# A planner that is told of a shorter latency between an operation and its dependents, and a layer boundary with another place in its queues

## The chip, the cores and the metric

The kernel runs on one core of a Trainium2 chip, as one program with one launch. The metric is the device time of one execution in microseconds (us), as the median of several runs; lower is better.

## What is computed

Two layers of a decoder trunk over 512 tokens of width 1024, batch 1, in float32. Cut to what matters:

```python
for l in range(DEPTH):                       # DEPTH = 2
    h = rms_norm(x, pre_norm_g[l])
    u = einsum('bsd,de->bse', h, w_in[l])    # 3424 columns, five groups
    # latent attention (MLA): low-rank query and key/value latents, rotary key
    q, k, v = from_latents(rms_norm(c_q) @ w_uq, rms_norm(c_kv) @ w_ukv)
    o_a = causal_softmax_attention(q, k, v)
    o_b = stick_breaking_attention(q, k, v)  # sigmoids, products from the right
    o_c = moba_attention(q, k, v, rel_bias)  # with 512 tokens plain causal softmax + bias
    o_d = conformer_conv(u_conv)             # gate, 31 taps, layer norm, swish, pointwise
    y = concat([o_a, o_b, o_c, o_d]) * silu(u_gate)
    y = einsum('bse,ed->bsd', y, w_out[l])
    x = x + rms_norm(y, post_norm_g[l])
```

## The kernel before

All matrices are split into a high and a low part (`hH`, `hL` for the normalised input, `w` for weights, `yH`, `yL` for the mixed output), and every product is three matmuls. Tokens are in four tiles of 128 (`t` = 0 to 3). Weights come in units of 128 x 512: a DMA into one of three `raw` buffers, a cast on ACT (L358) that makes the high part, and a subtraction on DVE or POOL (L363) that makes the low part. Six `w` buffers are used in turn.

No order of work is written out by hand. The program is a set of small tasks, written as generators. Each yields the engine that its next instruction needs, an estimated duration and the time at which its inputs are ready. `Flow.run` keeps a model of every engine's clock, and again and again issues the operation with the lowest key: its start in the model, plus a weight of the engine (`WT`: 0.078 for PE, 0.691 for DVE, 0.094 for POOL, 0 for ACT, 0.496 for SP) times the priority of its task (`PR`). What depends on an operation is taken to be ready at the operation's modelled end plus `LAG`. So the table of numbers sets the order in which instructions stand in each engine's queue, and each queue is then worked off in that order on the chip.

The names that matter:

- `x_new` (L1173 to L1197) closes a layer for one token tile: the square sum on ACT (L472), the sum and the power (L464 on DVE, L466 on POOL), four updates of `xt` on DVE (L1193). `boundary` (L519) normalises that tile for the next layer: another square sum (L472), L464, L466, then `h` on DVE (L527), transposes on PE (L537 `tr`), the split into `hH` on ACT (L544) and `hL` on DVE (L547).
- Products of the input projection: `lat` of a token tile (L580, 24 matmuls of 352 columns), the value chunk `vC` (L580 `acc`, 96 matmuls of 256 columns, 24 for a token tile), the others (L647, 512 columns, 24 for a half chunk).
- MLA's preparation: transposes of the latents (L693), `cq` from them (L760 on ACT, L762 on DVE), queries (L710, five matmuls a head), keys (L720) and values (L743), rotary embedding of queries on DVE or POOL (L779, L781, L786; L783 copies the rotary key). L720 and L743 use the weight unit `ukv`.
- Attention: scores (L1032 for MLA, L1037 otherwise) go to one of two PSUM buffers `sc`. DVE reads a score tile with the mask and takes the row maximum (L1064), ACT takes the exponential (L1072) and scales it (L1077), PE transposes the result (L1082), and L1098 multiplies with the values. A score buffer comes free when L1064 is through.
- The output projection is L1126. PE's other work is always issued as filler around attention.

Of the kernel before, what the change touches and what calls it, by code (L numbers as in the profile page):

```python
# [64 lines left out]
AORDER = (('mla', 0), ('mla', 1), ('moba', 0), ('moba', 1), ('sb', 0), ('sb', 1))  # L65


LAG = 330
CONV_NS = 205000.0
TAP_LATE = 40  # L70
TAP_EARLY = 100
# [3 lines left out]
BPN = 360.0  # L75
FBS = 1
SPARE0 = 1500.0
PR = {'low': 155, 'hs': 50, 'lat': 50, 'ev': 50, 'vev': 60, 'va': 65, 'cq': 40, 'q': 35, 'cn': -40, 'pw': -5, 'pv': 12, 'ys': 85, 'ye': 70, 'xn': 20, 'xs': 10, 'bd': 10, 'pre': 70, 'u0': 0, 'u1': 0, 'u2': 21, 'u3': 1}
BANKS = {"acc": 6, "sc": 2}
ENGINE = {"dvx": "dve", "plm": "pool"}  # L80
PORT = ("dvx", "pool")
# [8 lines left out]
class Flow:  # L90
# [19 lines left out]
    def spawn(self, prio, gen):  # L110
        task = [prio, self.n, gen, None]
        self.n += 1
        self.tasks.append(task)
        self.tasks.sort(key=lambda a: a[:2])
        self.resume(task, None)
# [7 lines left out]
    def run(self):  # L123
        while self.tasks:
# [17 lines left out]
            else:  # L142
# [6 lines left out]
                if len(q) > 3 and q[3]:  # L149
                    self.table = q[3]  # L150
                self.resume(task, (q[0], end + LAG) if isinstance(task[3], list) else end + LAG)

# [22 lines left out]
    def drop(self, buf, t):  # L175
        buf.at = max(buf.at, t)
        buf.uses -= 1
        if buf.uses == 0:
            self.free[buf.tag].append((buf.at, buf.idx))
            if buf.also:  # L180
                self.drop(buf.also, buf.at)
# [31 lines left out]
def trunk(ctx, tc, x, pre_g, w_in, w_sm, vecs, w_out, post_g, rel_bias, consts, onehot, out):  # L213
# [119 lines left out]
    def splitter():  # L333
        for key, src, n, nu, nk, w1 in feed:
            for kq in range(nu):
                raw, t0 = yield lambda: fl.ev.get(("raw", key, kq))
                r3 = raw.ap.rearrange("p (k c) -> p k c", k=nk)
                if w1:
                    raw.uses = nk
                    for j in range(nk):  # L340
# [4 lines left out]
                        A.copy(bh.ap, r3[:, j, :])  # L345
                        spawn(PR["low"], low_part(key, k, raw, r3[:, j, :], bh.ap, bl.ap, n, max(t, bl.at), [bh, bl]))
                else:
# [10 lines left out]
                    A.copy(wH, r3)  # L358
                    spawn(PR["low"], low_part(key, kq, raw, r3, wH, wL, 2 * n, t, b))

    def low_part(key, i, raw, r3, h, lo, n, t, b):
        e, t = yield from either(n, t)
        e.tensor_tensor(lo, r3, h.bitcast(F32), ALU.subtract)  # L363
        drop(raw, t)
        units[key, i] = (h, lo, t, b)
# [69 lines left out]
    def warm_up():  # L435
# [3 lines left out]
        while ("h", 0, 0, 0) not in fl.ev or fl.clock[pEng] < fl.ev["h", 0, 0, 0] - 600:  # L439
            te = yield pEng, 107 if t > WARM_AT else 213, t  # L440
            PE.matmul(b.ap[:, :256], zb[:, :P], zb[:, P : P + 256], start=True, stop=True)
            t = te - LAG
        drop(b, te)
# [88 lines left out]
    def flip_h(l, t, a, h, hp, tt, nb=4):  # L532
# [6 lines left out]
        sl = (slice(None), slice(a * nb, a * nb + nb), slice(t * P, (t + 1) * P))  # L539
        spawn(PR["hs"] + (0 if l else FBS) * t, h_split(l, t, a, nb, sl, tr3, tr, tp))  # L540

    def h_split(l, t, a, nb, sl, tr3, tr, tp):
        te = yield aEng, act(nb * P), tp
        A.copy(hs[0][sl], tr3)  # L544
        mark(("hH", l, t, a), te)
        te = yield vEng, dve(nb * P), te
        V.tensor_tensor(hs[1][sl], tr3, hs[0][sl].bitcast(F32), ALU.subtract)  # L547
        drop(tr, te)
        if nb < 4:
            mark(("hL", l, t, a), te)  # L550
            if ("hL", l, t, a ^ 1) in fl.ev:
                h_done(l, t, a // 2, te)
        else:
            h_done(l, t, a, te)

    def first_latents():
# [9 lines left out]
        for n, (k, x_, i) in enumerate(seq):  # L566
# [3 lines left out]
            PE.matmul(o, hs[x_][:, k, :P], (wh, wl)[i], start=n == 0, stop=n == len(seq) - 1)  # L570
        spawn(PR["lat"], latent_norm(0, 0, a, te))

    def tok_mm(o, wf, l, t, r, last):
        tc_ = slice(t * P, (t + 1) * P)
        for k in range(KT):
            th = yield from wait(("h", l, t, k // 4))
            wh, wl, tw, b = yield from wf(k)
            for i, (a, w) in enumerate(((hs[0], wh), (hs[0], wl), (hs[1], wh))):
                te = yield pEng, pe(wh.shape[-1]), max(th, tw, r)
                PE.matmul(o, a[:, k, tc_], w, start=k == 0 and i == 0, stop=k == KT - 1 and i == 2)  # L580
            last(k, b, te)
        return te

    def latents(l, t):
# [12 lines left out]
        te = yield from tok_mm(o, wf, l, t, a.at, last)  # L597
        spawn(PR["lat"], latent_norm(l, t, a, te))

    ckv = {}  # L600

    def latent_norm(l, t, a, te):
        zb = yield from take("qk", f"ckv{t}", C_SB)
        z = zb.ap
        t0 = yield aEng, act(C_SB), max(te, zb.at)
        A.copy(z, a.ap[:, :C_SB])
        drop(a, t0)
        ss = small("ssl", 2)
        jk = yield from take("yt", "jk", QR)
        t1 = yield aEng, acta(QR), max(t0, jk.at)  # L610
        A.activation(jk.ap, z[:, :QR], AF.Square, accum_out=ss[:, 0:1], scale=1.0 / math.sqrt(QR))
        t1 = yield aEng, acta(KVR), t0
        A.activation(jk.ap[:, :KVR], z[:, QR + RD :], AF.Square, accum_out=ss[:, 1:2], scale=1.0 / math.sqrt(KVR))
        drop(jk, t1)
        t2 = small("kr", 2 * RD, 2)
        kr = z[:, QR : QR + RD]
        tcs = yield from wait("cst")
        t0 = max(t0, tcs)
        td = yield xEng, 100, t0
        V.tensor_tensor(t2[:, :RD], kr, ck[:, t, :], ALU.mult)  # L620
        td = yield xEng, 85, t0
        V.tensor_tensor(t2[:, RD : RD + 16], kr[:, 16:], sk[:, t, 0:16], ALU.mult)
        td = yield xEng, 85, t0
        V.tensor_tensor(t2[:, RD + 16 :], kr[:, :16], sk[:, t, 16:], ALU.mult)
        r, t1 = yield from rsq(ss, 2, 1.0, t1)
        td = yield xEng, 100, td
        V.tensor_tensor(kr, t2[:, :RD], t2[:, RD:], ALU.add)
        td = yield xEng, dve2(QR), t1
        V.tensor_scalar(z[:, :QR], z[:, :QR], r[:, 0:1], None, ALU.mult)
        td = yield xEng, dve2(KVR), t1  # L630
        V.tensor_scalar(z[:, QR + RD :], z[:, QR + RD :], r[:, 1:2], None, ALU.mult)
        ckv[l, t] = zb
        mark(("ckv", l, t), td)

    def feat_chunk(l, c, evac, pre=None):
        key = (l, c)
        for m in range(2):
# [4 lines left out]
            for k in range(KT):  # L642
# [5 lines left out]
                if m == 1:  # L648
                    drop(b, te)
            spawn(PR["ev"], evac(m, a, te))  # L650

# [703 lines left out]
```

## Time and profile before

| | |
|---|---|
| median of 3 runs | 546.67 us (546.61 to 549.04) |
| the profiled execution | 547.47 us |
| its span, first to last instruction | 545.7 us |
| outside the span | 1.8 us |
| mean granted TensorE clock | 0.994 |
| PE busy | 532.7 us |
| DVE, ACT, POOL busy | 407.4, 362.8, 214.6 us |

The profiled execution is 0.8 us longer than the median. "Busy" counts a matmul from its start to its modelled end, so that the engine's pace is better read from the distance between two starts.

### The profile page before, as it was taken

The page shows a single profiled execution, that of the slowest core. Times are in us where ns is not written, and L with a number is a line of the kernel's source. Part 1 is how long each engine was busy: PE and PEld are TensorE (multiplying, and loading weights), DVE is VectorE, ACT ScalarE, POOL GpSimd, SP SyncE. Part 2 cuts the span into 40 slices and gives each one's busy share as a digit, 9 for nine tenths or more (in the row PEclk, how much of TensorE's full clock was granted, in tenths as well). Part 3 has the DMA queues.
Part 4 walks back from the last instruction along what each step waited for, and adds up shares of the span by engine and source line. Part 5 has one row for each costly group of instructions (what it writes and reads, how often), then busy time and mean ns, then how long its engine had stood idle before and what let it go on. Part 6 is the DMA issues. An engine that isn't in the chain of part 4 may idle for free.

```text
span 545.7 us, 9448 instructions
## 1 busy us (share of the span) xinstructions
PE 532.7 (98%) x3181; PEld 461.6 (85%) x3181; DVE 407.4 (75%) x914; ACT 362.8 (66%) x862; POOL 214.6 (39%) x255
## 2 busy tenths in 40 slices
PE   9999899999999999999998999999999999999995
PEld 5998678888888898899997967788888889989995
DVE  4667875788999988953687597558899998897243
ACT  5647898348995748654674699825699766674531
POOL 5823111572435643422241032048424566243321
PEclk9999899999999999999999999999999999999999
DMA  7423230344314263133763112323452423413245
GB/s 283 151 94 111 79 96 23 95 134 124 109 40 118 76 171 107 40 111 99 264 187 118 40 38 68 107 78 83 129 152 62 114 80 94 138 40 98 61 165 178
DMA packets 31025, 59.47 MB, mean 109 GB/s; under 512 B 4033, under 2 KB 5953, under 8 KB 30978
## 3 DMA queue, kind: packets, MB, share of 16 engines
q1 hardware_dynamic: 30978, 58.88, 35.8%
q8 instruction: 25, 0.41, 0.3%
q14 instruction: 22, 0.18, 0.1%
HBM read 49.17 MB, written 5.51 MB: 100 GB/s over the span
## 4 chain that ended last, share of the span: by engine, by line
PE 89%; DVE 5%; ACT 2%; POOL 1%; issue 1%; DMA 1%; SPq 0%; POOLq 0%; DVEq 0%; ACTq 0%
PE acc L647 40%; PE acc L1126 16%; PE acc L580 8%; PE pv L1098 5%; PE lat L580 5%; PE tr L1082 5%; PE sc L1037 4%; PE sc L1032 2%; DMA raw<-in_w_in_dram 1%; PE acc L968 1%; POOL wl L363 1%; DVE kT L783 1%; PE tr L537 1%; PE acc L710 1%; DVE qT L786 1%
## 5 line engine op out<-in xcount | busy, mean ns | idle before, releaser
L647 PE MATMUL acc<-hH,w 128*128 128x512 f32 x640 | 212.1, 403 | 0.0
L363 POOL TENSOR_TENSOR w<-raw,w 128x512 fp32r<-128x512 f32 x85 | 110.4, 1305 | 151.7 <-ACT w L358 126.2
L647 PEld LDWEIGHTS acc<-hH,w 128*128 128x128 f32 x640 | 119.5, 189 | 24.0 <-issue 0.4
L647 PE MATMUL acc<-hL,w 128*128 128x512 f32 x320 | 129.8, 406 | 0.0
L358 ACT CAST w<-raw 128x512 fp32r<-128x512 f32 x130 | 79.8, 622 | 42.1 <-PE acc L647 16.8
L893 DVE SCALAR_TENSOR_TENSOR cv<-cx,vec,cv 128x512 f32<-128x512 f32 x116 | 87.1, 751 | 2.4
L1126 PE MATMUL acc<-w,yH 128*128 128x256 f32 x416 | 75.3, 282 | 0.0
L647 PEld LDWEIGHTS acc<-hL,w 128*128 128x128 f32 x320 | 60.5, 189 | 11.4
L1126 PEld LDWEIGHTS acc<-w,yH 128*128 128x128 f32 x416 | 64.5, 189 | 0.4
L1126 PE MATMUL acc<-w,yL 128*128 128x256 f32 x208 | 59.0, 284 | 0.2
L363 DVE TENSOR_TENSOR w<-raw,w 128x512 fp32r<-128x512 f32 x45 | 33.4, 743 | 26.8 <-ACT w L358 26.7
L580 PE MATMUL acc<-w,hH 128*128 128x256 f32 x256 | 49.3, 287 | 1.9 <-DVE w L363 1.9
L382 DVE TENSOR_TENSOR pt<-tr,pt 128x128 fp32r<-128x128 f32 (+3 forms) x96 | 45.6, 484 | 5.8 <-ACT pt L376 4.5
L1082 PE MATMUL tr<-cst,p 128*128 128x128 f32 x240 | 42.2, 276 | 0.6 <-ACT p L1077 0.6
L580 PEld LDWEIGHTS acc<-w,hH 128*128 128x128 f32 x256 | 40.1, 189 | 2.8 <-DVE w L363 2.1
L376 ACT CAST pt<-tr 128x128 fp32r<-128x128 f32 (+3 forms) x96 | 39.8, 423 | 3.8 <-PE tr L1082 2.7
L1082 PEld LDWEIGHTS tr<-cst,p 128*128 128x128 f32 x240 | 30.2, 141 | 13.5 <-ACT p L1077 4.8
L1126 PEld LDWEIGHTS acc<-w,yL 128*128 128x128 f32 x208 | 39.3, 189 | 0.7 <-DVE yL L379 0.7
L580 PE MATMUL acc<-w,hL 128*128 128x256 f32 x128 | 36.4, 284 | 0.0
L1077 ACT ACTIVATE p<-p,s 128x128 f32<-128x128 f32 (+3 forms) x64 | 35.2, 562 | 1.8 <-DVE s L1075 1.8
L1072 ACT ACTIVATE p<-zb,s 128x128 f32<-128x128 f32 (+2 forms) x64 | 35.9, 561 | 0.3
L1161 POOL TENSOR_TENSOR yr<-yr,g 128x512 f32<-128x512 f32 x12 | 16.6, 1387 | 39.0 <-ACT jk L472 39.0
(179 smaller groups left out, 1019.8 us busy)
## 6 DMA issues: line engine op xcount, KB each, us to landing
raw<-in_w_in_dram SPq DMA_DIRECT2D x96, 256.0 KB, 2.7
raw<-in_w_out_dram SPq DMA_DIRECT2D x32, 256.0 KB, 2.6
xt<-in_x_dram SPq DMA_DIRECT2D x8, 512.0 KB, 4.2
raw<-in_w_sm_dram SPq DMA_DIRECT2D x8, 256.0 KB, 3.7
bias<-scratch SPq DMA_DIRECT2D x8, 256.0 KB, 2.9
m<-m SPq DMA_DIRECT2D x16, 128.0 KB, 3.2
b<-b SPq DMA_DIRECT2D x16, 128.0 KB, 2.8
x<-xt SPq DMA_DIRECT2D x4, 512.0 KB, 2.9
```

The lines of the kernel that those rows point to most:

```text
L358: A.copy(wH, r3)
L363: e.tensor_tensor(lo, r3, h.bitcast(F32), ALU.subtract)
L376: A.copy(dh, src)
L382: V.tensor_tensor(dl, src, dh.bitcast(F32), ALU.subtract)
L580: PE.matmul(o, a[:, k, tc_], w, start=k == 0 and i == 0, stop=k == KT - 1 and i == 2)
L647: PE.matmul(a.ap, w[:, cs], h[:, k, :], start=k == 0 and i == 0, stop=k == KT - 1 and i == 2)
L893: V.scalar_tensor_tensor(o.ap if j == CW - 1 else a.ap, xc[:, j : j + S], vc[:, w0 : w0 + 1], a.ap, ALU.mult, ALU.add)
L1072: A.activation(p.ap[:, :wd], src.ap[:, :wd], AF.Exp, bias=nm[:, 0:1], scale=-1.0, accum_out=ls)
L1077: A.activation(p.ap[:, :wd], p.ap[:, :wd], AF.Copy, scale=r[:, 0:1])
L1082: PE.transpose(tr3[:, j, :], p.ap[:, j * P : (j + 1) * P], ident)
L1098: PE.matmul(pv.ap[: (HD if i else P), j * P :], lhs, pt[i].ap[:, 4 * j * P : (3 * j + NT) * P], start=not i and not j, stop=(i, j) == PVSE ...
L1126: PE.matmul(o, a[:, k, tc_], w, start=first and i == 0, stop=stop and i == 2)
```

## The change

Two numbers of the planner are set anew; no operation of the program is added or removed except some of the warm-up matmuls at the start, and ACT, DVE and POOL share the weight subtractions and rotary products otherwise than before.

```diff
-LAG = 330
+LAG = 200
...
-PR = {..., 'xs': 10, 'bd': 10, 'pre': 70, ...}
+PR = {..., 'xs': 10, 'bd': -40, 'pre': 70, ...}
```

`LAG` is added to every dependency in the planner's model, in nanoseconds. `bd` is the priority of the tasks `boundary` and `first_boundary`; a lower number is earlier. All queues are reordered by it. Three places follow, rows as the built programs have them.

DVE in layer 0, when MLA's queries of heads 0 and 1 (`qT0`, `qT1`) get their rotary embedding. Before (`w_636` is the weight unit `ukv`):

```order
L363 TENSOR_TENSOR w_636<-raw_350,w_636 128x512
L413 COPY ebias_653<-pb_655 128x512
L779 TENSOR_TENSOR qT0_643<-rt_673,cst_72 32x512
L781 TENSOR_TENSOR rt_673<-rt_673,cst_72 32x512
L783 COPY kT0_644<-cq_579 32x512
L786 TENSOR_TENSOR qT0_643<-qT0_643,rt_673 32x512
L779 TENSOR_TENSOR qT1_674<-rt_687,cst_72 32x512
L382 TENSOR_TENSOR vC_251<-acc_553,vC_251 128x8x64
L1064 ISA zb_744,s8_743<-sc_724,mask_82 128x128
```

DVE at the same place in the changed program (`w_654` is now the unit `ukv`):

```order
L779 TENSOR_TENSOR qT0_618<-rt_640,cst_72 32x512
L781 TENSOR_TENSOR rt_640<-rt_640,cst_72 32x512
L783 COPY kT0_619<-cq_558 32x512
L786 TENSOR_TENSOR qT0_618<-qT0_618,rt_640 32x512
L779 TENSOR_TENSOR qT1_641<-rt_653,cst_72 32x512
L363 TENSOR_TENSOR w_654<-raw_348,w_654 128x512
L781 TENSOR_TENSOR rt_653<-rt_653,cst_72 32x512
L783 COPY kT1_642<-cq_558 32x512
L786 TENSOR_TENSOR qT1_641<-qT1_641,rt_653 32x512
L382 TENSOR_TENSOR vC_234<-acc_595,vC_234 128x8x64
L1064 ISA zb_735,s8_734<-sc_714,mask_82 128x128
```

The low part of `ukv` has moved from ahead of the rotary work of head 0 to behind the first product of head 1.

PE at that place. Before, the second pair of MLA heads, with scores of head 0 (`sc_757`, `sc_765`) in both buffers and those of head 1 (`sc_804`) next:

```order
L1032 MATMUL sc_757<-kT0_644,qT0_643 128x512
L1032 MATMUL sc_765<-kT0_644,qT0_643 128x384
L710 MATMUL acc_740<-cq_576,w_393 128x512
L710 MATMUL acc_785<-cq_574,w_393 128x512
L710 MATMUL acc_785<-cq_575,w_393 128x512
L710 MATMUL acc_785<-cq_574,w_393 128x512
L710 MATMUL acc_785<-cq_576,w_393 128x512 x2
L720 MATMUL acc_798<-cq_577,w_636 128x512
L720 MATMUL acc_798<-cq_578,w_636 128x512
L720 MATMUL acc_798<-cq_577,w_636 128x512
L647 MATMUL acc_708<-hH_83,w_648 128x512
L1032 MATMUL sc_804<-kT1_675,qT1_674 128x128
```

PE in the changed program, where `ukv` is first used and the first scores of both heads follow:

```order
L580 MATMUL acc_595<-w_293,hL_84 128x256
L720 MATMUL acc_700<-cq_556,w_654 128x512
L720 MATMUL acc_700<-cq_557,w_654 128x512
L720 MATMUL acc_700<-cq_556,w_654 128x512
L743 MATMUL acc_723<-w_654,cq_556 128x256 x2
L743 MATMUL acc_723<-w_654,cq_557 128x256
L743 MATMUL acc_723<-w_654,cq_556 128x256 x2
L743 MATMUL acc_723<-w_654,cq_557 128x256
L743 MATMUL acc_730<-w_654,cq_556 128x256 x2
L1032 MATMUL sc_714<-kT0_619,qT0_618 128x128
L1032 MATMUL sc_715<-kT0_619,qT0_618 128x256
```

The long scores of head 0 no longer stand ahead of the short ones of head 1; they come later, behind 26 matmuls of L647. Between the first queries (ten matmuls of L710) and the first L720 there are now 27 of L580.

DVE at the layer boundary, around the third and fourth weight unit of `vC` of layer 1. Before (`xt_3510` is token tile 3, `w_3639` and `w_3646` are the two units):

```order
L363 TENSOR_TENSOR w_3639<-raw_3572,w_3639 128x512
L464 TENSOR_REDUCE s8_3687<-ss0_80 128x1
L1181 TENSOR_TENSOR yl_3679<-acc_3512,g2_2534 128x256
L547 TENSOR_TENSOR hL_84<-tr_3670,hH_83 128x4x128
L527 SCALAR_TENSOR_TENSOR h_3696<-xt_3449,s8_3620,g2_2534 128x512
L1193 SCALAR_TENSOR_TENSOR xt_3510<-yr01_3048,s8_3688,xt_3510 128x256
L1193 SCALAR_TENSOR_TENSOR xt_3510<-yr11_3181,s8_3688,xt_3510 128x256
L1193 SCALAR_TENSOR_TENSOR xt_3510<-yr21_3448,s8_3688,xt_3510 128x256
L1193 SCALAR_TENSOR_TENSOR xt_3510<-yl_3679,s8_3688,xt_3510 128x256
...
L631 TENSOR_SCALAR ckv1_3649<-ckv1_3649,s8_3699 128x128
L363 TENSOR_TENSOR w_3646<-raw_3612,w_3646 128x512
```

DVE in the changed program (`w_3539`, `w_3553`, `w_3592`, `w_3601` are the four units of `vC`; `ss0` holds the square sums of tile 2, `xt_3455` is tile 2):

```order
L363 TENSOR_TENSOR w_3553<-raw_3542,w_3553 128x512
L629 TENSOR_SCALAR ckv0_3565<-ckv0_3565,s8_3585 128x192
L631 TENSOR_SCALAR ckv0_3565<-ckv0_3565,s8_3585 128x128
L363 TENSOR_TENSOR w_3592<-raw_3550,w_3592 128x512
L363 TENSOR_TENSOR w_3601<-raw_3563,w_3601 128x512
L464 TENSOR_REDUCE s8_3637<-ss0_80 128x1
L620 TENSOR_TENSOR kr_3649<-ckv1_3619,cst_72 128x32
L622 TENSOR_TENSOR kr_3649<-ckv1_3619,cst_72 128x16
L1181 TENSOR_TENSOR yl_3621<-acc_3457,g2_2544 128x256
L624 TENSOR_TENSOR kr_3649<-ckv1_3619,cst_72 128x16
L310 TENSOR_SCALAR s8_3662<-s8_3628 128x2
L1193 SCALAR_TENSOR_TENSOR xt_3455<-yr01_3044,s8_3638,xt_3455 128x256
```

All four units of `vC` now stand ahead of the updates of tiles 2 and 3. On PE the first transposes of tile 2 (`tr`, L537) stood behind 3 matmuls of `vC`; now they stand behind 40.

## Rows read from the trace of the kernel before

**Rows 1.** The page's first part: busy time of each engine.

```profile
PE 532.7 (98%) x3181; PEld 461.6 (85%) x3181; DVE 407.4 (75%) x914; ACT 362.8 (66%) x862; POOL 214.6 (39%) x255
```

**Rows 2.** Windows of PE: start:end, us, busy us, granted clock, DMA.

```profile
44.60:62.80 18.20, 16.29 (x75) 0.91 0.32 94
...
270.50:309.40 38.90, 36.56 (x276) 1.00 0.39 125
309.40:332.60 23.20, 22.23 (x113) 1.00 0.20 57
```

**Rows 3.** PE's waits by releaser: us in total, times, longest.

```profile
PE sc L1032 <- DVE s L1064: 2.5, 2, 1.9
PE acc L580 <- DVE w L363: 1.9, 1, 1.9
```

**Rows 4.** The chain that ended last: start us, us, what.

```profile
17.18 3.85 PE lat L580 x24
...
33.83 2.36 PE acc L580 x20
...
94.78 30.77 PE acc L647 x133
```

**Rows 5.** Timelines of PE, DVE and POOL in layer 0's MLA: start us, us, instruction.

```profile
44.64 2.45 PE L710 MATMUL acc<-cq,w 128*128 128x512 f32 x10
...
48.98 0.68 DVE L786 TENSOR_TENSOR qT<-qT,rt 32x512 f32<-32x512 f32 x1
49.59 0.68 DVE L779 TENSOR_TENSOR qT<-rt,cst 32x512 f32<-32x512 f32 x1
...
52.31 2.92 POOL L363 TENSOR_TENSOR w<-raw,w 128x512 fp32r<-128x512 f32 x2 [0.20 <-ACT w L358]
53.99 1.78 DVE L786 TENSOR_TENSOR qT<-qT,rt 32x512 f32<-32x512 f32 x1
55.51 0.39 PE L647 MATMUL acc<-hH,w 128*128 128x512 f32 x1
57.81 0.49 PE L1032 MATMUL sc<-kT,qT 96*128 96x128 f32 x2 [1.91 <-DVE s L1064]
```

**Rows 6.** The window of PE just behind that wait, columns as in rows 2.

```profile
58.40:61.80 3.40, 3.40 (x11) 0.50 0.01 2
```

**Rows 7.** Timelines of PE and DVE at the layer boundary, tile 2 and `vC`.

```profile
288.04 0.28 PE L580 MATMUL acc<-w,hL 128*128 128x256 f32 x1
288.79 0.63 PE L537 MATMUL tr<-cst,h 128*128 128x128 f32 x4 [0.47 <-DVE h L527]
289.17 0.36 PE L580 MATMUL acc<-w,hH 128*128 128x256 f32 x1
...
290.67 0.68 DVE L363 TENSOR_TENSOR w<-raw,w 128x512 fp32r<-128x512 f32 x1
...
291.41 0.38 PE L580 MATMUL acc<-w,hH 128*128 128x256 f32 x1 [1.87 <-DVE w L363]
```

**Rows 8.** Timelines of ACT and PE, tile 3: first square sum and first transposes.

```profile
285.79 0.38 ACT L472 ACTIVATE jk<-acc 128x256 f32<-128x256 f32 x1 [0.46 <-PE acc L1126]
...
294.12 0.60 PE L537 MATMUL tr<-cst,h 128*128 128x128 f32 x4
```

**Rows 9.** Timelines of PE and DVE in layer 1's MLA.

```profile
304.84 1.47 PE L693 MATMUL tr<-cst,ckv 128*128 128x128 f32 x12
...
307.49 1.53 DVE L762 SCALAR_TENSOR_TENSOR cq<-tr,vec,cq 64x512 fp32r<-64x512 f32 x2 [0.54 <-ACT cq L760]
...
319.32 0.61 PE L720 MATMUL acc<-cq,w 128*128 128x512 f32 x2
320.32 0.33 PE L1082 MATMUL tr<-cst,p 128*128 128x128 f32 x1 [0.39 <-ACT p L1077]
...
324.84 0.47 PE L647 MATMUL acc<-hL,w 128*128 128x512 f32 x1
325.89 0.91 PE L1032 MATMUL sc<-kT,qT 96*128 96x384 f32 x2 [0.58 <-DVE s L1064]
```

More of the change, by code (lines that the diff above doesn't have):

```diff
@@ L77 @@
 SPARE0 = 1500.0
-PR = {'low': 155, 'hs': 50, 'lat': 50, 'ev': 50, 'vev': 60, 'va': 65, 'cq': 40, 'q': 35, 'cn': -40, 'pw': -5, 'pv': 12, 'ys': 85, 'ye': 70, 'xn': 20, 'xs': 10, 'bd': 10, 'pre': 70, 'u0': 0, 'u1': 0, 'u2': 21, 'u3': 1}
+PR = {'low': 155, 'hs': 50, 'lat': 50, 'ev': 50, 'vev': 60, 'va': 65, 'cq': 40, 'q': 35, 'cn': -40, 'pw': -5, 'pv': 12, 'ys': 85, 'ye': 70, 'xn': 20, 'xs': 10, 'bd': -40, 'pre': 70, 'u0': 0, 'u1': 0, 'u2': 21, 'u3': 1}
 BANKS = {"acc": 6, "sc": 2}
```

## The prediction

> **What bounds the kernel now.** I read the page's first part, then PE in windows, then PE's waits, then timelines at the few places where PE waits. PE is busy 98% of the span [rows 1], and the change neither adds nor removes work that matters: four bf16 warm-up matmuls fewer, at a point where PE waits for the first inputs anyway. So the time can change only through the time that PE loses, and the reader should look for that alone; waits of DVE, ACT and POOL count where PE waits behind them. PE's pace without waits comes from the chain: 30.77 / 133 = 0.231 us for a matmul of 512 columns, 2.36 / 20 = 0.118 for one of 256, 3.85 / 24 = 0.160 for a latent one [rows 4]. Three stretches lose time: layer 0's MLA, the layer boundary, and layer 1's MLA, where busy time falls short of the window by 1.9, 2.3 and 1.0 us [rows 2]. The waits by releaser say for what: scores wait for DVE's L1064, which frees a score buffer, and `vC` waits for a weight unit from DVE [rows 3]. Layer 0 has a cost beside it: the granted clock in that window is 0.91 [rows 2].
>
> **What the change does, and the terms of the sum.**
>
> *The lag itself.* DVE's subtraction of 0.68 us starts at 290.67, and PE, which waited for it, starts at 291.41: 0.74 us from start to start [rows 7]. The planner counts 0.601 + 0.330 = 0.93 for that, and 0.80 with the new lag. On this link 200 is nearer, so the new order asks for dependents earlier, but not earlier than they can come. The lag moves all queues. The priority `bd` weighs little: 50 units are 0.078 x 50 = 4 ns of key on PE and 0.691 x 50 = 35 ns on DVE. The order agrees: tiles 0 and 1 come forward by 7 to 14 PE places, and tile 2 goes back, from 3 `vC` matmuls ahead of its transposes to 40. I count orders, not intentions.
>
> *Layer boundary.* Before, PE lost (288.79 - 288.04) - 0.118 = 0.63 us for `h` of tile 2, and (291.41 - 289.17) - 0.118 = 2.12 us for the last unit of `vC`, whose subtraction stood behind tile 3's updates on DVE [rows 7]. Together 2.75. Now all four units stand ahead of the updates, so the 2.12 go. What is late next is `h` of tile 2 and 3. Tile 3's chain took 294.12 - 285.79 = 8.3 us from its first square to its transposes, waits in queues included [rows 8]. The new cover of tile 2 is 24 + 40 matmuls of 256 columns, 64 x 0.118 = 7.55 us; of tile 3 it is 59 such matmuls, eight transposes and ten latent ones, 7.0 + 0.8 + 1.6 = 9.4. By the whole 8.3, tile 2 waits 0.8, tile 3 not at all; part of the 8.3 was queueing, so I take 0.4 in all (bounds 0 and 0.8). A second new wait: the latents' transposes to the last `cq` took 304.84 to 307.49 + 1.53 = 309.02, 4.2 us [rows 9]. Now 12 transposes (1.2), 8 matmuls of 256 (0.94) and 6 of 512 columns (1.39) cover 3.5 of it, and L710 waits 0.65 (bounds 0 and 0.9). Term: 2.75 - 0.4 - 0.65 = **1.7 us gained** (1.05 to 2.75).
>
> *Layer 0's MLA.* Before, PE stood for 1.91 us ahead of `sc` at 57.81 [rows 5]: both buffers held long scores of head 0, and DVE's queue ahead of L1064 had been stretched; L786, 0.68 us at 48.98, took 1.78 at 53.99, while POOL did two subtractions in 2.92 us. After that wait the clock is at 0.50 for 3.40 us [rows 6], 1.2 GHz instead of 2.4, which costs half, 1.7 us. Loss 3.6. In the new order short scores of both heads come first, and 26 matmuls of L647 stand ahead of the long ones: this wait goes. But `ukv` (`w_654`) is now subtracted behind `qT1`'s first product. From L710's start at 44.64 that product ended at 49.59 + 0.68, 5.6 us later [rows 5]. `w_654` then takes 0.7, so L720 can start at 6.3 at best, or at 7.6 if one POOL subtraction gets in between (1.46 each by the row of two). PE arrives after 10 x 0.231 + 27 x 0.118 = 5.5. It waits 0.8 or 2.1; I take 2.0, as POOL's two units are cast right behind `ukv` on ACT. Then `sc` of head 1 needs L1064 behind three rotary operations and a value split: PE has about 2.6 us of work for some 3.7 us of DVE's, a wait of 1.1 (bounds 0 and 1.5). New loss 3.1 without a fall of the clock. Term: 3.6 - 3.1 = **0.5 us gained**. Bounds: -1.2 (the clock falls again) and +2.8 (0.8 and nothing).
>
> *Layer 1's MLA.* Before, PE lost (320.32 - 319.32) - 0.46 = 0.54 and (325.89 - 324.84) - 0.23 = 0.82 at two places [rows 9], 1.4 us. After, `ukv` is early here, as before. A score behind eight matmuls of L710 may wait 0.9 if POOL delays DVE as it did, 0 if not; the middle, and a little for transposes, make 0.6. Term: **0.8 us gained** (0 to 1.4).
>
> *The rest.* At the start the second power moves ahead of one POOL subtraction, and PE's transposes of tile 2 move forward with it: 0. In the middle of both layers, where L647 fills PE (the 30.77 us for 133 matmuls hold no gap [rows 4]), the order changes with no wait that I can name: 0, with 1 us to either side. The tail is the same, row by row.
>
> Sum: 1.7 + 0.5 + 0.8 = 3.0 us. Against the profiled execution, 547.47 - 3.0 = 544.5; that one is 0.8 above the median, so against the median 546.67 - 3.0 = **543.7 us**.
>
> **The rivals.**
>
> *The waits move rather than go.* A single wait of 1.91 us was followed by 3.40 us at half clock [rows 5, 6], and the new wait ahead of L720 is as long. If the clock falls again, 1.7 of the 3.0 are given back: 545.4. For it: the same length, at the same point of the stream. Against it: the 1.87 us at the boundary [rows 7] had no such fall, as the granted clock of 1.00 in that window shows [rows 2]. The second way to the same case is the port. L786 beside POOL took 1.1 us longer [rows 5]; if both POOL subtractions come ahead of `w_654`, the wait grows by 1.46, the term becomes -1.0, and the time 545.1. The Trainium skill, "SBUF — State Buffer", section "Who interferes with whom", has a rule for that: DVE and GpSimd share one port pair as an exclusive lock, and the loser is blocked for a whole instruction; the row agrees, as it exceeds neither 0.68 nor one POOL instruction on top. By that rule alone an estimate of this wait is 1.46 or 2.92, never a part.
>
> *A cleaner gain.* If `w_654` gets in ahead of POOL's first subtraction, L720 waits 0.8 and the rotary work is not stretched, so that the score wait shrinks with it: 2.3 more than the sum, and without the small new waits at the boundary 1.0 more: 540.4.
>
> *Slower: dependents that come too early.* With 130 ns less of margin at every link, a transposition L1082 may stand at the head of PE's queue before its row is scaled. PE works in order, so all filler behind it waits too. There are 96 groups of transposes (32 heads and tiles in each of three attentions). In the waits they do not appear among the long ones [rows 3]. If each waited 0.13 us, that would be 12.5 us; it decides against the kernel from 5.7 / 96 = 0.06 us a group. At 0.1 it would be 546.67 - 3.0 + 9.6 = 553.3. Against it: the link measured above is 0.74, under the 0.80 now counted.
>
> *Nothing of the kind.* That the change does nothing is excluded for the order, as all five queues differ.
>
> **How the numbers follow.** About 0.5% (2.7 us, so 543.9 and 549.4) is what a measurement of this kernel can tell from no change. The forecast, waits shrunk by about 3 us, has a chance of 0.53 and its own range is 541.5 to 545.3; two thirds of it lie below 543.9. The moved waits have 0.27, 545.1 to 547, nearly all within 0.5%. The cleaner gain has 0.08, near 540.4. The slower case has 0.12. Faster: 0.36 + 0.08 + a little of the moved ones, 0.47. Same: 0.17 + 0.24, 0.41. Slower 0.12. The range leaves out the slower case and half of the cleaner one: 540.6 to 547.2.
>
> **What would show it.** In the changed profile: no wait of `acc` L580 for `w` L363 at the boundary; waits of `tr` L537 and of L710 there under 1 us each; a wait of L720 for `w` L363 of 0.8 to 2.1 us about 5.5 us after the first L710 of layer 0; no score wait of 1.9 us behind it; the granted clock between there and the first values at 1.00 (forecast) or 0.5 for some us (moved waits). Waits of L1082 for ACT of over 4 us in total would show the slower case. The prediction is wrong if PE loses time in the middle of a layer, where I counted nothing, or if L720 never waits.

## The result, and the profile after

The changed kernel takes 555.32 us in the median of 4 runs (553.25 to 557.40), the kernel before 546.64 (546.41 to 549.04): a ratio of 1.0146, with a 95% interval of 1.0121 to 1.0172. It is 8.7 us slower, where 3 us faster was forecast. The profiled execution is the longest of the four (557.40 us); its span is 555.5 us, 9.8 more than that of before's profiled execution (547.47 us).

The page's first part answers to [rows 1]:

```profile
PE 538.5 (97%) x3177; PEld 462.1 (83%) x3177; DVE 419.8 (76%) x925; ACT 361.4 (65%) x860; POOL 205.5 (37%) x244
```

PE does four warm-up matmuls fewer and is busy 5.8 us longer, in part because matmuls ran at a lower clock, as the windows below show. DVE is busy 12.4 us longer. Eleven more instructions are part of that, but 5.8 us are the eight instructions of L929, which take 8.6 us in place of 2.8: a sign that they were held up while they ran. PE's waits by releaser (us in total, times, longest) answer to [rows 3]:

```profile
PE tr L938 <- DVE xn L929: 4.4, 6, 0.9
PE sc L1032 <- DVE s L1064: 2.0, 3, 1.3
PE acc L720 <- DVE w L363: 1.3, 1, 1.3
...
PE acc L647 <- DVE pt L382: 0.9, 1, 0.9
```

The wait of `vC` for L363 at the layer boundary is gone, as forecast, and L720 waits, as forecast. The first row is new. L929 is the scaling in the layer norm of the conformer branch (`conv_norm`): four instructions on DVE, one for each token tile, behind a power on POOL (L312). L938 are the eight transposes that follow on PE. Windows of PE (start:end, us, busy us, granted clock, DMA): layer 0's MLA, the first `conv_norm` and what follows it, the layer boundary, the second `conv_norm` and what follows it.

```profile
43.06:58.00 14.94, 12.38 (x75) 1.00 0.34 108
195.98:201.30 5.32, 3.12 (x21) 1.00 0.32 99
201.30:204.71 3.41, 3.41 (x19) 0.50 0.24 51
271.91:316.90 44.99, 44.50 (x337) 1.00 0.43 148
462.41:467.54 5.13, 2.92 (x19) 1.00 0.36 102
467.54:470.95 3.41, 3.41 (x18) 0.50 0.23 49
```

In each layer PE stands idle for 2.2 us of some 5 around L938, and behind that the granted clock is 0.50 (1.2 GHz of 2.4) for 3.41 us. The boundary is nearly without gaps now.

To put a number on every stretch I took each form of matmul at the commonest distance between two starts in before's trace (the paces of [rows 4], 0.108 us for a transposition and so on). Over the program, warm-ups left out, that is 516.5 us of work for every kernel here. (Which distance is taken for a form moves a whole column, by up to 1 us and in all rows alike; the differences between rows stay.) How much later a matmul starts than the work ahead of it says is what was lost by then. Growth of that loss by stretch, in us, of the profiled executions (L0 and L1 are the layers; experiments are explained below):

| | start | MLA L0 | to the conv norm | conv norm L0 | end of L0 | boundary | MLA L1 | middle L1 | conv norm L1 | rest | sum |
|---|---|---|---|---|---|---|---|---|---|---|---|
| work, us | 0-30 | 30-50 | 50-180 | 180-195 | 195-260 | 260-300 | 300-330 | 330-430 | 430-445 | 445- | |
| before | 8.42 | 4.29 | 1.38 | 0.11 | 1.09 | 2.96 | 2.37 | 1.08 | 0.08 | 1.16 | 22.9 |
| changed | 9.49 | 3.27 | 4.16 | 4.44 | 0.71 | 1.31 | 2.39 | 1.72 | 4.55 | 0.70 | 32.7 |
| e1, lag alone | 9.66 | 4.14 | 3.85 | 4.21 | 0.94 | 1.19 | 2.38 | 1.72 | 5.80 | 0.70 | 34.6 |
| e2, priority alone | 8.47 | 1.52 | 1.76 | 0.15 | 1.15 | 0.82 | 0.50 | 1.11 | 0.08 | 1.18 | 16.7 |
| e3, before + POOL | 8.45 | 2.68 | 1.82 | 1.99 | 1.14 | 4.50 | 2.47 | 1.12 | 1.98 | 1.16 | 27.3 |
| e4, changed, POOL behind | 9.03 | 3.29 | 4.08 | 0.15 | 1.38 | 1.30 | 2.40 | 1.70 | 0.35 | 0.71 | 24.4 |
| e5, changed, PE later | 9.68 | 3.27 | 4.25 | 2.20 | 2.10 | 1.33 | 2.03 | 1.69 | 2.14 | 2.33 | 31.0 |

Of the 9.8 us between the first two rows, 8.8 lie at the two conv norms. The timelines of DVE, POOL and PE (start us, us, instruction) show what happens there. Rows are left out where a line of dots stands. This is the changed kernel, in the upper rows in layer 0's MLA, where POOL was forecast to hold DVE up, in the lower rows at the first conv norm:

```profile
48.06 3.45 POOL L363 TENSOR_TENSOR w<-raw,w 128x512 fp32r<-128x512 f32 x2 [6.45 <-ACT w L358]
48.71 1.65 DVE L363 TENSOR_TENSOR w<-raw,w 128x512 fp32r<-128x512 f32 x1
50.40 1.66 DVE L781 TENSOR_TENSOR rt<-rt,cst 32x512 f32<-32x512 f32 x1
50.42 0.50 PE L720 MATMUL acc<-cq,w 128*128 128x512 f32 x1 [1.25 <-DVE w L363]
...
54.19 0.46 PE L1032 MATMUL sc<-kT,qT 96*128 96x128 f32 x2 [1.31 <-DVE s L1064]
...
193.86 1.58 POOL L312 TENSOR_TENSOR s<-s,mhalf 128x4 f32<-128x4 f32 x1 [1.71 <-DVE s L310]
195.98 4.29 DVE L929 TENSOR_SCALAR xn<-xn,s,s 128x256 f32<-128x256 f32 x4
196.25 3.87 POOL L363 TENSOR_TENSOR w<-raw,w 128x512 fp32r<-128x512 f32 x3
...
196.96 0.27 PE L938 MATMUL tr<-cst,xn 128*128 128x128 f32 x1
197.78 0.33 PE L938 MATMUL tr<-cst,xn 128*128 128x128 f32 x1 [0.55 <-DVE xn L929]
199.05 0.33 PE L938 MATMUL tr<-cst,xn 128*128 128x128 f32 x1 [0.94 <-DVE xn L929]
...
200.33 0.77 PE L938 MATMUL tr<-cst,xn 128*128 128x128 f32 x5 [0.72 <-DVE xn L929]
```

The same place in the kernel before:

```profile
199.29 1.01 POOL L312 TENSOR_TENSOR s<-s,mhalf 128x4 f32<-128x4 f32 x1 [1.98 <-DVE s L310]
200.33 1.39 DVE L929 TENSOR_SCALAR xn<-xn,s,s 128x256 f32<-128x256 f32 x4 [1.12 <-POOL s L312]
...
201.59 0.38 PE L938 MATMUL tr<-cst,xn 128*128 128x128 f32 x2
...
206.52 1.36 POOL L363 TENSOR_TENSOR w<-raw,w 128x512 fp32r<-128x512 f32 x1 [6.23 <-ACT w L358]
```

Before, POOL has nothing to do beside L929, whose four instructions take 1.39 us. After, three of POOL's weight subtractions (L363, 3.87 / 3 = 1.29 us each) start 0.27 us behind the first L929, and the four take 4.29. The transposes behind them come 1.27 and 1.28 us apart (197.78, 199.05, 200.33): the length of one POOL instruction.

### The profile page after: what moved, and what is told of

Its sections match the earlier page's. It is cut to its first block, busy times and chain, and to the rows that moved or that the text cites. A ratio compares the mean times of both kernels' runs of the same rounds, so it can differ in the third digit from the quotient of the medians.

```text
span 555.5 us, 9404 instructions
## 1 busy us (share of the span) xinstructions
PE 538.5 (97%) x3177; PEld 462.1 (83%) x3177; DVE 419.8 (76%) x925; ACT 361.4 (65%) x860; POOL 205.5 (37%) x244
## 4 chain that ended last, share of the span: by engine, by line
PE 77%; DVE 8%; ACT 8%; DMA 3%; issue 2%; SPq 0%; POOL 0%; POOLq 0%; DVEq 0%; ACTq 0%
PE acc L647 32%; PE acc L1126 15%; PE acc L580 7%; PE pv L1098 4%; PE lat L580 4%; PE tr L1082 4%; PE sc L1037 3%; DMA xt<-in_x_dram 2%; PE sc L1032 2%; ACT p L1072 2%; DVE xn L929 2%; ACT p L1077 2%; ACT pt L376 1%; PE tr L537 1%; PE acc L968 1%
## 5 line engine op out<-in xcount | busy, mean ns | idle before, releaser
L647 PE MATMUL acc<-hH,w 128*128 128x512 f32 x640 | 215.5, 404 | 0.9 <-DVE pt L382 0.9
L363 POOL TENSOR_TENSOR w<-raw,w 128x512 fp32r<-128x512 f32 x80 | 104.6, 1315 | 147.3 <-ACT w L358 144.1
L647 PEld LDWEIGHTS acc<-hH,w 128*128 128x128 f32 x640 | 118.3, 188 | 25.0 <-DVE pt L382 1.2
L647 PE MATMUL acc<-hL,w 128*128 128x512 f32 x320 | 127.2, 398 | 0.0
L1126 PE MATMUL acc<-w,yH 128*128 128x256 f32 x416 | 75.0, 282 | 0.0
L647 PEld LDWEIGHTS acc<-hL,w 128*128 128x128 f32 x320 | 60.3, 188 | 11.5 <-issue 0.2
L1126 PEld LDWEIGHTS acc<-w,yH 128*128 128x128 f32 x416 | 64.4, 189 | 0.2
L1126 PE MATMUL acc<-w,yL 128*128 128x256 f32 x208 | 58.6, 282 | 0.0
L363 DVE TENSOR_TENSOR w<-raw,w 128x512 fp32r<-128x512 f32 x50 | 38.0, 775 | 26.6 <-ACT w L358 25.9
L580 PE MATMUL acc<-w,hH 128*128 128x256 f32 x256 | 50.6, 294 | 0.0
L580 PEld LDWEIGHTS acc<-w,hH 128*128 128x128 f32 x256 | 42.5, 201 | 0.7 <-issue 0.5
L1082 PE MATMUL tr<-cst,p 128*128 128x128 f32 x240 | 42.3, 277 | 0.1
L1082 PEld LDWEIGHTS tr<-cst,p 128*128 128x128 f32 x240 | 29.9, 140 | 14.4 <-ACT p L1077 5.7
L1126 PEld LDWEIGHTS acc<-w,yL 128*128 128x128 f32 x208 | 39.3, 189 | 0.0
L580 PE MATMUL acc<-w,hL 128*128 128x256 f32 x128 | 37.8, 295 | 0.1
L1077 ACT ACTIVATE p<-p,s 128x128 f32<-128x128 f32 (+2 forms) x64 | 35.2, 563 | 0.8 <-DVE s L1075 0.7
```

The source lines that it names most:

```text
L647: PE.matmul(a.ap, w[:, cs], h[:, k, :], start=k == 0 and i == 0, stop=k == KT - 1 and i == 2)
L1077: A.activation(p.ap[:, :wd], p.ap[:, :wd], AF.Copy, scale=r[:, 0:1])
L1082: PE.transpose(tr3[:, j, :], p.ap[:, j * P : (j + 1) * P], ident)
L1126: PE.matmul(o, a[:, k, tc_], w, start=first and i == 0, stop=stop and i == 2)
```

## The experiments

The theory was then: POOL's subtractions beside L929 cost the two conv norms, PE stands behind them, and the clock falls (the port theory). Its rival: with a shorter lag the planner puts L938 too close behind its input on PE, and POOL has no part in it. Ratios are to runs of the kernel before on the same chip. Those had medians from 547.4 to 548.1 us, so times from different chips are best compared by their ratios.

**e1 and e2: which of the two numbers.** Each makes one of these two edits in the kernel before.

```diff
-LAG = 330
+LAG = 200
...
-PR = {..., 'bd': 10, ...}
+PR = {..., 'bd': -40, ...}
```

> LAG = 200 alone, bd stays 10. The trace of the changed kernel loses 4.4 us in each layer at the transposes L938 of the conformer's layer norm. Port theory: this is because three of POOL's weight subtractions (L363) stand right behind the power (L312) and run beside DVE's scaling L929; in this kernel the same POOL rows stand there, so L929 x4 takes about 4.3 us in place of 1.4 and both losses stay: 555 +- 2, whatever the boundary does. Rival, the priority bd is what costs: near the kernel before, 545 to 548.

> bd = -40 alone, LAG stays 330. Port theory: POOL's rows around the power are those of the kernel before (one subtraction behind it, whose cast on ACT comes much later), so L929 x4 takes 1.4 us and PE loses nothing at L938: 546.7 +- 2, from small waits elsewhere. Rival, bd is what costs: 553 or more.

e1: 559.16 us, ratio 1.0213 (1.0198 to 1.0229). e2: 541.71 us, ratio 0.9897 (0.9883 to 0.9912). The lag does all the harm, and more than the change as a whole shows (11.8 us against 8.7); POOL's three rows stand behind the power in e1 and L938 waits 4.4 us, as in the changed kernel. e2 fell below its expectation: the priority alone gains 5.7 us and beats both kernels. The two don't simply add up: 11.8 lost and 5.7 gained would be 6.1 slower, and the change is 8.7 slower. The waits of e2 on PE are few:

```profile
PE warm L441 <- POOL warm L432: 1.0, 1, 1.0
PE sc L1032 <- DVE s L1064: 0.7, 1, 0.7
PE tr L537 <- DVE h L527: 0.5, 1, 0.5
```

**e3: the kernel before, with three instructions on POOL.**

```diff
-        rr, tr_ = yield from rsq(vr, NT, 1.0, td)
+        rr, tr_ = yield from rsq(vr, NT, 1.0, td); [G.tensor_tensor(ca[l, 0].ap, mask[:, :S], mask[:, :S], ALU.subtract) for _ in range(3)]
```

> The kernel before, with three subtractions of 128x512 on POOL added right behind the power L312 in both layers, which nobody reads; PE, DVE, ACT and SP keep their order row by row. Port theory: L929 x4 stretches from 1.39 to about 4.3 us; PE reaches the last L938 about 2.2 us too early in each layer: 546.7 + 4.4 = 551 if the granted clock stays, and 554.5 if it falls to 0.50 for 3.4 us behind each wait as in the changed kernel. Rival, the shorter lag by itself has put L938 too close behind its input on PE and POOL has no part in it: 546.7 +- 0.7, L929 unchanged.

552.59 us, ratio 1.0098 (1.0081 to 1.0115): slower by 5.2. Timeline of the first conv norm, and two windows of PE:

```profile
199.14 3.26 POOL L926 TENSOR_TENSOR ca<-mask 128x512 f32<-128x512 f32 x3
199.19 3.68 DVE L929 TENSOR_SCALAR xn<-xn,s,s 128x256 f32<-128x256 f32 x4 [1.12 <-POOL s L312]
...
201.49 0.33 PE L938 MATMUL tr<-cst,xn 128*128 128x128 f32 x1 [0.72 <-DVE xn L929]
...
202.61 0.33 PE L938 MATMUL tr<-cst,xn 128*128 128x128 f32 x1 [0.55 <-DVE xn L929]
```

```profile
55.00:62.00 7.00, 5.09 (x23) 1.00 0.24 73
292.64:296.05 3.41, 3.41 (x14) 0.50 0.84 247
```

With all other queues unchanged, POOL alone stretches L929 from 1.39 to 3.68 us and costs 2.0 us at each conv norm, where before lost 0.1. (About 4.3 us were expected of L929; but the three instructions added take 3.26 us, the subtractions of the changed kernel 3.87.) The time lies between the two that the theory gave, 551 and 554.5; the rival would have given 546.7 and falls. In the profiled execution, the fastest of the four, the granted clock didn't fall at the conv norms. But it fell at the layer boundary, and not behind the score wait in layer 0, where before's execution had it [rows 6]; that wait is 1.9 us in both.

**e4: the changed kernel, with POOL held behind L929.** One small copy on POOL reads the last scaled tile; the planner holds the subtractions back until it is in the queue.

```diff
-        self.port = []
+        self.port = []; self.hold = False
...
-        rr, tr_ = yield from rsq(vr, NT, 1.0, td)
+        fl.hold = True; rr, tr_ = yield from rsq(vr, NT, 1.0, td)
...
-        cs = []
+        td = yield mEng, 70, tz[-1]; G.tensor_copy(small("hx"), xn[NT - 1][:, :1]); fl.hold = False; cs = []
...
-        e, t = yield from either(n, t)
+        yield lambda: None if fl.hold else 0; e, t = yield from either(n, t)
```

> The changed kernel, with one copy of 128x1 on POOL that reads the last scaled tile and stands ahead of POOL's subtractions, so that these start only when L929 is through; on PE L938 moves back by three matmuls of 256 columns (0.35 us), all other queues keep their order. Port theory: L929 x4 takes 1.4 us again, L938 waits under 0.5 us, the clock doesn't fall there: 555.3 - 2 x 4.4 = 546.5 (545.5 to 548). Rival, L938 stands too early on PE: 0.35 us a layer is all that comes back, 554.6.

548.48 us, ratio 1.0019 (1.0001 to 1.0036). Timeline of DVE and POOL:

```profile
195.44 1.43 DVE L929 TENSOR_SCALAR xn<-xn,s,s 128x256 f32<-128x256 f32 x4
...
196.94 0.45 POOL L930 COPY s<-xn 128x1 f32<-128x1 f32 x1 [1.19 <-DVE xn L929]
197.34 3.78 POOL L363 TENSOR_TENSOR w<-raw,w 128x512 fp32r<-128x512 f32 x3
```

L929 is back at 1.43 us, no wait for L929 is left on PE, the clock doesn't fall there, and the two conv norms lose 0.15 and 0.35 us instead of 4.44 and 4.55. So POOL's subtractions beside L929 are what costs the change its conv norms. The time is 2 us above the expected 546.5, 0.5 over its upper bound, and still 6.8 above e2: the lag loses elsewhere too. By the table that is 1.8 us in layer 0's MLA, 2.3 between it and the first conv norm, and 1.9 in layer 1's MLA; no run takes these apart.

**e5: the changed kernel, with L938 later on PE.**

```diff
-                te = yield pEng, 107, max(tz[t], tr.at)
+                te = yield pEng, 107, max(tz[t] + 3500, tr.at)
```

> The changed kernel, in which the planner takes the scaled tiles to be ready 3.5 us later for PE alone: some 23 matmuls of 256 columns (2.7 us) and three between the transposes move ahead of L938's; three of POOL's subtractions stay behind the power. It asks whether DVE's stretched L929 costs by itself or only through PE standing at L938. Only through PE: L929 x4 still takes about 4.3 us, L938 waits under 1 us in all of a layer, no fall of the clock behind it, and the time is that of the run with POOL's work behind L929, 548.5 +- 1.5. By itself (what follows on DVE is late as well): 551 or more.

555.11 us, ratio 1.0138 (1.0108 to 1.0168): no gain. The edit moved more than it should: two of POOL's subtractions run beside L929 instead of three, so it takes 3.39 us and not 4.29. Timeline of DVE and PE:

```profile
196.22 3.39 DVE L929 TENSOR_SCALAR xn<-xn,s,s 128x256 f32<-128x256 f32 x4
199.53 0.55 DVE L1057 TENSOR_TENSOR p<-p,cs 128x384 f32<-128x384 f32 x1
...
200.22 0.52 PE L1082 MATMUL tr<-cst,p 128*128 128x128 f32 x3 [1.76 <-DVE p L1057]
```

L938 waits no more, but the instruction behind L929 on DVE is late too, and now L1082 waits for it, 1.76 us. The stretch costs by itself, whoever stands behind it. The conv norms lose 2.2 each, without a fall of the clock. The ends of the layers lose 1.4 and 1.6 more than in the changed kernel, and in layer 0 the trace shows the same clash at another place: at 233.74 a L1057 on DVE takes 1.63 us, where 0.55 is usual for its size, beside a L363 on POOL (233.50, 1.45 us), and L1082 waits 1.13 us for it.

**e6 to e8, e11 and e12: other lags, with bd = -40.** Each changes the one line to 260, 360, 400, 325 and 340.

> LAG = 260, bd = -40. Theory of the margin (a shorter lag leaves PE less room everywhere, so time falls steadily with a longer lag): between 548.5 (200, without the port loss) and 541.7 (330), so about 545. Theory of the rows (what counts is which instructions come to stand side by side, and the lag only shuffles them): three subtractions of POOL stand right behind the power here, with ten matmuls of 256 columns more ahead of L938's than in the changed kernel, so PE loses 2 to 4 us a layer there: 549 to 554 with the other waits.

> LAG = 360, bd = -40, a longer lag than the kernel before has. Theory of the margin: no more than at 330, 540 to 542. Theory of the rows: three subtractions of POOL stand right behind the power here too; if their casts on ACT are done by then, L929 stretches to about 4.3 us and PE loses 2 to 4 us a layer: 546 to 550.

> LAG = 400, bd = -40. No subtraction of POOL stands behind the power. Both theories: 540 to 543, without a wait at L938; over 545 would mean that a longer lag has a cost of its own elsewhere.

> LAG = 325, bd = -40, 5 ns from the best run. Margin or any smooth effect of the lag: 541.7 +- 0.7. Theory of the rows (each value gives another order, and the other numbers of the table were chosen beside 330): any place up to 551; no subtraction of POOL but one whose cast comes late stands behind the power, so no loss at L938.

> LAG = 340, bd = -40, 10 ns from the best run on the other side. Smooth effect: 541.7 +- 0.7 (at 360 it was 556.3, so a smooth curve would give up to 546). Theory of the rows: any place from 541 to 556; no loss at L938, since one subtraction alone stands behind the power.

| LAG | 200 | 260 | 325 | 330 | 340 | 360 | 400 |
|---|---|---|---|---|---|---|---|
| median, us | 555.32 | 553.75 | 542.22 | 541.71 | 546.70 | 556.26 | 554.62 |
| ratio | 1.0146 | 1.0107 | 0.9909 | 0.9897 | 0.9981 | 1.0142 | 1.0124 |
| interval | 1.0121-1.0172 | 1.0075-1.0140 | 0.9885-0.9933 | 0.9883-0.9912 | 0.9963-0.9999 | 1.0095-1.0188 | 1.0091-1.0157 |

The theory of the margin falls: 360 and 400 are as slow as 200. The theory of the rows isn't shown by this either: its ranges were wide, and 360 and 400 lie outside them. Waits of PE by releaser at 260, 360 and 400:

```profile
PE tr L1082 <- DVE p L1057: 3.9, 4, 1.5
PE tr L938 <- DVE xn L929: 2.9, 4, 0.9
```

```profile
PE acc L1126 <- DVE w L363: 3.6, 2, 1.8
PE sc L1032 <- DVE s L1064: 2.9, 2, 1.5
```

```profile
PE acc L1126 <- ACT yH L376: 2.8, 2, 1.4
PE acc L1126 <- DVE yL L379: 2.7, 4, 0.9
```

At 260 the loss lies at the conv norms again (4.4 us a layer, counted as in the table above), but at 360 and 400 it lies at the end of the layers, where the output projection L1126 waits for its weights or inputs: 6.6 and 6.5 us a layer, falls of the clock included. For e7 the place that I had named was a small part (L938 waits 1.4 us), and the time is 6 us above its range. In layer 0 the loss begins with the same clash there: two L379 on DVE take 1.78 us beside a L363 on POOL (232.02, 1.27 us), the weight's subtraction stands behind them on DVE, and L1126 waits 1.78 us for it. For e8 both theories missed by 12 us; there L1126 waits for the mixed output, and why that comes late is open. Among the values tried, the time is flat between 325 and 330, at 340 it is 5 us up, at 260 and 360 over 12.

**e9 and e10: other priorities, with LAG = 330** (bd = -10 and -80).

> bd = -10, LAG = 330. Theory of the priority (normalisation ahead of other work is what gains, so it gains with any earlier place): 541 to 544, with the gains of bd = -40 at the layer boundary (loss 0.8 us in place of 2.9) and in both layers' MLA. Theory of the rows (bd only shuffles them; the gain of -40 is of that one order): somewhere between 541 and 551, the boundary and MLA not alike between -10 and -40.

> bd = -80, LAG = 330. Theory of the priority: 541 to 543, no worse than -40. Theory of the rows: between 541 and 551, with waits at other places than at -40. POOL's order is that of bd = -40 row by row, so by both no loss at L938.

542.23 us (0.9906, 0.9877 to 0.9935) and 542.03 (0.9905, 0.9880 to 0.9929). All three values gain alike and lose the same 0.8 to 0.9 us at the boundary. So the gain doesn't hang on the value. The three orders are near to one another on PE, though (3,103 and 3,114 of 3,156 matmuls stand in e2's sequence; of the kernel before, 2,951), so they are not three independent samples. e11, at 325, has only 2,953 in common with e2 and gains as much, which speaks against one lucky order.

**e13 and e14: the priority for one layer's tasks.**

```diff
-            spawn(PR["bd"] + (1 if l else FBS) * t, boundary(l, t) if l else first_boundary(t))
+e13         spawn((PR["bd"] if l else -40) + (1 if l else FBS) * t, boundary(l, t) if l else first_boundary(t))
+e14         spawn((-40 if l else PR["bd"]) + (1 if l else FBS) * t, boundary(l, t) if l else first_boundary(t))
```

> bd = -40 for the first layer's boundary tasks alone, LAG = 330; up to the layer boundary this is the order of the run with bd = -40 row by row. That run's trace loses 2.8 us less in layer 0's MLA (no score wait of 1.9 us, no fall of the clock behind it). If the gain arises in each place by itself: 546.7 - 2.8 = 543.9 +- 1, with the boundary losing 2.1 us more than with -40 for all. If one order gains as a whole or not at all: 546 to 548 or 541.7.

> bd = -40 for the second layer's boundary tasks alone, LAG = 330; the order is that of the kernel before row by row up to the boundary. If the gain arises in each place by itself: the boundary's 2.1 us and layer 1's MLA 1.6 us, 546.7 - 3.7 = 543.0 +- 1, with the wait of scores in layer 0 unchanged at 1.9 us. If it came from the start alone: 546.7 +- 0.7.

e13: 546.39 us, ratio 0.9970 (0.9956 to 0.9984). e14: 543.66 us, ratio 0.9912 (0.9888 to 0.9937). The kernel before ran at 548.12 beside them. e14 gains 4.5 us, at the boundary (2.96 to 0.88 us lost) and in layer 1's MLA (2.37 to 0.54), each as expected and in its own place. e13 gains 1.7 us where 2.8 were expected, and its time lies above its range: it gains in layer 0's MLA (4.29 to 1.53), but its start loses 0.6 more, and in its profiled execution the clock falls at the boundary instead, as in e3: 4.46 lost there in place of 2.96.

## Why the prediction was wrong

**The step that failed is "The rest".** It says that in the middle of both layers the order changes "with no wait that I can name: 0, with 1 us to either side". There the change lost 8.8 us, at the two conv norms: L929 on DVE took 4.29 us in place of 1.39, because three of POOL's subtractions ran beside it, and PE stood behind it and then ran at a lower clock. With the start and the smaller losses below, the places priced at 0 lost 12.4 us (9.8, and the 2.65 gained in the three places that were priced). The step looked for gaps in before's trace alone. It didn't go through the new order for places where POOL's instructions had come to stand beside DVE's, though POOL's rows of both kernels showed it: behind the power L312, one subtraction whose cast came 6 us later before, and three ready ones after. In the planner's own clock the two don't overlap: `start` pushes a subtraction of POOL and the DVE operations marked `dvx`, to which L929 belongs, out of each other's way. But nothing in the program holds them there, and on the chip POOL goes on as soon as its own inputs are ready. e3 puts such a cost in with no other queue changed, and e4 takes it out.

**The rival of the port was right in kind and at the wrong place.** I let POOL's subtractions delay `ukv` only. They did: L363 on DVE took 1.65 us beside POOL, L720 waited 1.25 us and the scores 1.31, where 2.0 and 1.1 were forecast. (One sum behind the 2.0 is a little short: 6.3 + 1.46 is 7.8 and not 7.6.) The estimate that such a wait is a whole POOL instruction, "never a part", didn't hold: L363 took 1.65 us where 0.68 is usual, 0.97 more, and POOL's two took 3.45. Nor does the row that it rested on show a whole one: L786 was 1.10 over its 0.68, where POOL's instruction took 1.46. The Trainium skill, "SBUF — State Buffer", section "Who interferes with whom", says that a `tensor_scalar` can take the port pair that DVE shares with GpSimd, that whoever issues first has it for a whole instruction, and that the other is blocked meanwhile. L929 is a `tensor_scalar`, and the trace agrees: behind the first, its instructions end one POOL instruction apart, 1.27 to 1.28 us against 1.29. Asked of every place and not of one, that rule would have pointed at L929.

**The slower rival** said that transposes would stand at PE's head before their input was there, and that is what was seen. But it meant 96 groups of L1082 at 0.1 us, and it was two groups of L938 at 2.2 us, with the clock behind them. That its 553.3 us came near 555.3 is chance.

**The lag itself.** "200 is nearer" rested on one link of 0.74 us. The runs show that nearness on a link isn't what decides: of the seven values tried, 325 and 330 are fastest, and the time rises on both sides. At 200 there are small losses beside the conv norms (start 1.1 us, from layer 0's MLA to the conv norm 2.8, middle of layer 1 0.6), and e4 still has most of them (0.6, 2.7 and 0.6). What makes each of them wasn't taken apart.

**"The priority weighs little"** also failed. In its place e2 shows 5.7 us from the priority alone. 4 ns of key is little as a time, but in the planner's code PE's ready operations all have PE's clock as their start, so they tie, and then any difference decides. That this is why -10, -40 and -80 gain alike is argued from the planner's rule; that they do is shown by e9 and e10. That the gains at the boundary and in layer 1 arise by themselves is shown by e14; for layer 0's, e13 shows it in the trace but not in the time.

**Point by point.** Layer boundary: 1.7 forecast, 2.96 - 1.31 = 1.65 measured; the wait for L363 is gone and that of `tr` is 0.4, as forecast, but the wait of L710, forecast at 0.65, didn't come, so the agreement is in part luck. Layer 0's MLA: 0.5 forecast, 4.29 - 3.27 = 1.02 measured; no fall of the clock there, as forecast. Layer 1's MLA: 0.8 forecast, nothing measured; only the priority alone gained there (e2, 1.9). All these terms would have been gained with the old lag, and more of them: e2 has 2.1, 2.8 and 1.9 in the three places, in this order. The conditions under which I called myself wrong (lost time in the middle of a layer) are the ones that came. The range missed because it counted no place but those where PE already waited.

## What to carry to other kernels

When a change permutes queues, list in the new order every place where one engine's instructions have come beside another's that share something with it, also where the old trace shows no wait: a planner's clock keeps them apart only on paper, unless a dependency does. A wait that an edit takes away in one place says nothing about what the same edit makes elsewhere, so price two numbers apart: here one alone gained 5.7 us and the other alone lost 11.8. The best value of a planner's constant can lie in a narrow place (here 325 and 330 of seven values), and nearness to a measured latency didn't find it.

## What the runs showed of the hardware

With three of POOL's L363 waiting, one instruction of L929 on DVE got through for each of POOL's, and not all four behind all three: each but the first ended 1.27 to 1.28 us behind the one ahead, where they are 0.32 us apart alone. POOL kept its own pace: three in 3.87 us, 1.29 each, and two in 2.54 at 194.77 in the kernel before, 1.27 each. With a `tensor_tensor` on DVE in L929's place both gave way: in layer 0's MLA DVE's L363 took 1.65 us in place of 0.68, and POOL's two took 3.45.

A wait of the same length has different consequences: before's execution stood 1.9 us for the scores in layer 0 and had a clock of 0.50 behind it [rows 6], and 1.9 us at the boundary with the clock at 1.00 [rows 2]; e3's, with the same waits, had it the other way round. Such a fall cost less than the half of 3.41 us that the prediction took: at the conv norms matmuls of 256 columns started 0.213 us apart in it and 0.118 otherwise, which by these figures is an estimate of 1.5 us. Single executions of one order differ by about that much: e14 took 542.36 us at a mean clock of 0.998, and 543.75 in the profiled execution, at 0.996, which has one such fall in layer 0's MLA.
